# Three edits to a two-block transformer kernel on one core: wide FFN matmuls, 64-row scores, differential attention filled in pieces

## Chip, core and metric

One NeuronCore of a Trainium2 chip runs the whole program in one launch. The metric is the device time of that launch in microseconds (us); lower is better. The kernel is written in Python with a tile framework, which orders the instructions of each engine when it builds the program. The engines are TensorE (PE, its weight loads PEld), VectorE (DVE), ScalarE (ACT), GpSimd (POOL) and SyncE (SP, which issues the DMAs). Each takes its instructions strictly in the order in which they stand, except that PE may load weights ahead.

## The reference, cut to what matters

`x` is 256 tokens of width 1024, `ctx` another 256. The first block mixes by convolution and retention, then has a feed forward (2816 wide) and a gated side input. The second block has two layers over `x` and `ctx`. The parts that the change touches:

```python
f = (silu(h @ w_ffn_gate) * (h @ w_ffn_up)) @ w_ffn_down        # block 1; layer 2 of block 2 has the same form, x alone
# layer 1 of block 2: differential attention, 8 heads, each of two 64-wide halves m
s = einsum('bqhmd,bkhmd->bhmqk', q_blk, k) * 64 ** -0.5
p = softmax(s);  p = p[:, :, 0] - lam * p[:, :, 1];  o = p @ v   # x attends to ctx and x, ctx to ctx
y = (rmsnorm(o) * subln * 0.8) @ wo                              # norm per head
# layer 2 of block 2: neighbourhood attention, 16 heads of 64, x alone as queries
s = concat([q @ k_band * 64 ** -0.5 + bias, q @ k_ctx * 64 ** -0.5]);  o = softmax(s) @ v
```

All is float32.

## The kernel before

**Number format.** A float32 matrix is held as two parts, `hi` (rounded to the format float32r that PE multiplies in one pass) and `lo` (the rest). A product is three float32r matmuls per 128-row slice k of the contraction: weight hi by x hi, weight hi by x lo, weight lo by x hi (`mm3`, lines 156 to 163; `mm3_tok`, lines 165 to 172, has the tokens as the stationary side). Each of the three loads its own 128x128 weights. Weights come from memory as float32; `weights` (line 121) loads a tile `raw` of 128x1024, ACT casts it to `hi` (line 129) and DVE subtracts to get `lo` (line 130). Four `raw` and five `hi` and `lo` buffers let this run ahead of PE.

**Feed forwards.** The one of block 1 (22 steps j, lines 563 to 588) and the one of layer 2 (lines 1107 to 1118) have 256 tokens. Per j, gate and up are each 8 slices k of `mm3` with 256 (or, in layer 2, 258) columns; the result is scaled on DVE out of PSUM (line 574, line 1113), ACT takes silu, DVE multiplies, and `split` (line 146) makes the two parts. In layer 2 two extra columns carry the shift of the norm, and the scale of the norm is multiplied in afterwards. `down` (line 590) then takes 22 slices k per output block n, eight blocks. The feed forward of layer 1 (lines 965 to 985) has x and ctx side by side, 512 columns, and is not touched. Into these stages the framework also moves `ada_dve` (line 243): 320 multiplies of 128x512 on DVE that make the modulation vectors and are needed only later.

**Differential attention** (lines 725 to 866). For each c of 4, q, k and v of two heads are projected from `xl` (x) while the parts of `ctx` were done earlier for c below 3 (`early_qk`, `early_v`, line 637). `rope` (line 728) is four DVE operations of 256 columns. Then come 8 units (`da_unit`, line 744), 32 in all: one head, one half of 128 queries, over 512 keys (x queries) or 256 keys (ctx queries). A unit is two score matmuls `s` of 64 contraction rows, one for each half m, on plain float32 (line 757); per m a maximum on DVE (761), its scaling by -1/8 (762) and the exponential on ACT (764); the combination on DVE (767 to 770); transposes on PE (773); a copy by ACT (775); the products with v (780); the norm of the head (783 to 787, with one `pow` on POOL); and a transpose `on` that is put off by one unit (`flush`, 742). The two score banks of PSUM (`pss`) are the only two. The output projection by the first six heads, for x (`wo_first(0)`, line 901), stands after all units.

**Neighbourhood attention** (lines 983 to 1077). A score `s` of a head and 128 queries is two matmuls: one of 128 rows, in which the other head's 64 rows hold the low part of q (line 989), and one of 64 rows for the low part of k (line 990). To make these packed tiles q and k are copied in halves of 64 partitions (lines 1039 to 1041 and 1069 to 1070).

**Order.** The framework chooses the order on each engine by a model of its own, within data dependencies and the hints `tc.issue_after(x)` (not before x).

Of the kernel before, what the change touches and what calls it, by code (L numbers as in the profile page):

```python
# [35 lines left out]
EARLYN = 9  # L36
# [25 lines left out]
def body(ctx, tc, a):  # L62
# [91 lines left out]
    last_mm = [None]  # L154

    def mm3(out, w, xs, first=True, last=True):
# [408 lines left out]
    rc_ = stc.rstd()  # L565
    ada = AdaPE(ADA_PE)
    fs = []
    for j in range(KF):
        w = w_blocks(a["ffn1"][j])
        ps = bank(pmm, "mm")  # L570
        for i in range(2):
            mm3(ps[:, i * T:(i + 1) * T], w[i], xs)
        gu = tmp2()
        op = dve.tensor_tensor(
            gu.rearrange("p (j t) -> p j t", j=2), ps.rearrange("p (j t) -> p j t", j=2),
            rx[:, :T].unsqueeze(1).to_broadcast([P, 2, T]), op=ALU.mult)
        if j == 1:
            in_ffn = last_load[0], op.ins
        sg = tmp1()
        act.activation(sg, gu[:, :T], AF.Silu)  # L580
        dve.tensor_tensor(sg, sg, gu[:, T:], op=ALU.mult)
        s = slot("x" if ring(j) == "pt" else ring(j), F32R)
        split(sg, s[:, :T], s[:, T:])
        fs.append((s[:, :T], s[:, T:]))
# [5 lines left out]
    def down(name, fs, epilogue):  # L590
        for n in range(KD):
            ps = bank(pmm, "mm")
            for hf in range(2):
                w = per_k(weights(a[name][2 * n + hf], (6 * P, 5 * P)), (6, 5), P)
                mm3(ps[:, :T], w, fs[hf * KH:(hf + 1) * KH], first=hf == 0, last=hf == 1)
            epilogue(n, ps)
# [25 lines left out]
    def ep(n, ps):  # L622
# [9 lines left out]
        st.add(ps[:, :T])  # L632
# [3 lines left out]
        act.activation(s[:, (n % 2) * T:(n % 2 + 1) * T], ps[:, :T], AF.Copy, scale=col(V_FFNPOST, n))  # L636
# [3 lines left out]
    early = [], [], []  # L640

    def early_qk(c, grp):
        w = w_blocks(a["wqkv0"][grp * 4 + c])
        ps = bank(pss, "s")
        for j in range(2):
            o = ps[:, j * T:(j + 1) * T]
            mm3(o, w[j], xc)
            if c < 2:
                s = slot("q")
                act.copy(s[:, T:], o)  # L650
                early[c].append(s)
        if c == 2:
            s = slot("o")
            act.copy(s, ps)
            early[c].append(s)

    def early_v(c):
# [4 lines left out]
        s = slot("q" if c < 2 else "o")  # L662
        act.copy(s, ps)
        early[c].append(s)

    steps = [lambda c=c, i=i: early_v(c) if i == 2 else early_qk(c, i) for c in range(3) for i in range(3)][:EARLYN]

# [49 lines left out]
    epsc = const.tile([P, 1], F32, name="epsc")  # L717
    dve.memset(epsc, EPS)
# [4 lines left out]
    dve.tensor_scalar(out=sub8, in0=col(V_SUBLN), scalar1=1.0 - LAM_INIT, scalar2=None, op0=ALU.mult)  # L723
# [21 lines left out]
    def da_unit(q, k, v, hh, ctx_q, qt, po_all, at):  # L745
# [7 lines left out]
        p, ps = [], []  # L753
# [505 lines left out]
```

## Time and profile before

| what | value |
|---|---|
| three runs | 1449.93, 1446.19, 1448.93 us; median 1448.93 |
| the profiled execution: time | 1450.36 us |
| its span, first to last instruction | 1448.1 us |
| PE, weight loads, DVE, ACT, POOL busy | 97%, 87%, 74%, 48%, 2% |
[...]
| chain that ended last | PE 80%, issue 13%, DMA 2%, DVE 2%, ACT 1% |
| DMA | 163 GB/s mean, its engines about half busy |

How to read it: matmuls are pipelined and the profile models their ends, so a matmul row of 0.28 us overlaps its successors, and PE reads as busy as soon as matmuls follow each other closely. What a matmul costs PE is seen in the start of the next one. The stages lie, from the span's start, about so: block 1 up to its feed forward 0 to 162, feed forward 162 to 350, the rest of block 1 and the early projections to 442, differential attention to 643, layer 1's output and feed forward to 1060, neighbourhood attention to 1240, its output and feed forward to the end.

### The profile page before, as it was taken

Reading aid. Unit: us, or ns where it says so; the run is one execution under the profiler, and the core shown is the slowest. Engines: PE = TensorE matmul, PEld = TensorE weight load, DVE = VectorE, ACT = ScalarE, POOL = GpSimd, SP = SyncE. Lnnn points to the kernel's source line nnn. Section 1 sums busy time; section 2 is a strip of 40 time slices with the busy share of each in tenths; the row PEclk is TensorE's granted clock in tenths of the full one; section 3 lists DMA queues with packets and bytes.
Section 4 is the critical chain, followed back from the end, with each engine's and each line's share of the span. In section 5 each row is a group of like instructions: output and inputs, shape, how many; then the busy total and the mean of one; then the engine's idle time right before and its main releaser. Section 6 shows DMA issues by size and latency. Waiting matters only on the chain.

```text
span 1448.1 us, 25617 instructions
## 1 busy us (share of the span) xinstructions
PE 1410.9 (97%) x9811; PEld 1262.8 (87%) x9811; DVE 1075.4 (74%) x2333; ACT 700.5 (48%) x1323; POOL 34.1 (2%) x52
## 2 busy tenths in 40 slices
PE   7998999999999999999999999999999999999997
PEld 6898899999998887589888888889988778899997
DVE  7975889985778785778699999965775576676653
ACT  5655544454554545754432222323565555654442
POOL 0000000000000010110000000000000000000000
PEclk9999899999999999999999999999999999999998
DMA  8457498677554331034466676634632233355562
GB/s 289 128 168 255 169 318 275 218 215 221 167 175 146 131 96 32 7 103 160 132 215 198 210 239 218 210 123 129 203 99 87 74 88 119 132 182 182 153 180 91
DMA packets 76874, 236.66 MB, mean 163 GB/s; under 512 B 8656, under 2 KB 13008, under 8 KB 76624
## 3 DMA queue, kind: packets, MB, share of 16 engines
q1 hardware_dynamic: 76752, 235.03, 50.6%
q8 instruction: 77, 1.26, 0.3%
q14 instruction: 45, 0.37, 0.1%
HBM read 233.95 MB, written 1.05 MB: 162 GB/s over the span
## 4 chain that ended last, share of the span: by engine, by line
PE 80%; issue 13%; DMA 2%; DVE 2%; ACT 1%; SPq 0%; POOL 0%; DVEq 0%; POOLq 0%; ACTq 0%
PE mm L161 19%; PE mm L162 19%; PE mm L163 19%; PE s L757 3%; PE mm L172 2%; PE mm L171 2%; PE mm L170 2%; PE t L780 2%; PE o L1022 1%; DMA raw<-w_in 1%; PE s L162 1%; PE s L161 1%; PE s L163 1%; PE t L1012 1%; PE s L990 1%
## 5 line engine op out<-in xcount | busy, mean ns | idle before, releaser
L129 ACT CAST hi<-raw 128x1024 fp32r<-128x1024 f32 (+2 forms) x376 | 358.8, 956 | 547.8 <-PE mm L162 345.7
L130 DVE TENSOR_TENSOR lo<-raw,hi 128x1024 fp32r<-128x1024 f32 (+2 forms) x376 | 415.5, 1106 | 158.1 <-ACT hi L129 154.6
L161 PE MATMUL mm<-x,hi 128*128 128x256 f32 (+2 forms) x1568 | 486.3, 314 | 13.0 <-ACT x L151 7.9
L162 PE MATMUL mm<-x,hi 128*128 128x256 f32 (+2 forms) x1568 | 487.4, 312 | 1.3 <-DVE x L612 1.0
L163 PE MATMUL mm<-x,lo 128*128 128x256 f32 (+2 forms) x1568 | 487.5, 312 | 0.8 <-DVE lo L130 0.8
L161 PEld LDWEIGHTS mm<-x,hi 128*128 128x128 f32 x1568 | 299.9, 193 | 39.7 <-issue 11.4
L163 PEld LDWEIGHTS mm<-x,lo 128*128 128x128 f32 x1568 | 301.9, 193 | 23.5 <-issue 8.6
L162 PEld LDWEIGHTS mm<-x,hi 128*128 128x128 f32 x1568 | 301.9, 193 | 22.2 <-issue 6.1
L256 DVE SCALAR_TENSOR_TENSOR junk<-adaw,sb 128x512 f32<-128x512 f32 x320 | 220.2, 688 | 12.9 <-DMA adaw<-ada 8.5
L161 PE MATMUL mm<-o,hi 128*128 128x256 f32 (+1 forms) x356 | 105.3, 300 | 0.7 <-ACT o L147 0.5
L162 PE MATMUL mm<-o,hi 128*128 128x256 f32 (+1 forms) x356 | 105.6, 298 | 0.0
L163 PE MATMUL mm<-o,lo 128*128 128x256 f32 (+1 forms) x356 | 105.3, 297 | 0.0
L163 PE MATMUL s<-x,lo 128*128 128x258 f32 (+1 forms) x288 | 81.9, 284 | 0.0
L161 PE MATMUL s<-x,hi 128*128 128x258 f32 (+1 forms) x288 | 81.8, 284 | 0.0
L162 PE MATMUL s<-x,hi 128*128 128x258 f32 (+1 forms) x288 | 81.8, 284 | 0.0
L162 PE MATMUL mm<-q,hi 128*128 128x256 f32 (+1 forms) x265 | 81.0, 306 | 0.0
L163 PE MATMUL mm<-q,lo 128*128 128x256 f32 (+1 forms) x265 | 80.9, 305 | 0.0
L161 PE MATMUL mm<-q,hi 128*128 128x256 f32 (+1 forms) x265 | 80.9, 305 | 0.0
L161 PEld LDWEIGHTS mm<-o,hi 128*128 128x128 f32 x356 | 67.4, 191 | 5.4 <-issue 1.7
L162 PEld LDWEIGHTS mm<-o,hi 128*128 128x128 f32 x356 | 68.0, 191 | 2.6 <-issue 0.5
L163 PEld LDWEIGHTS mm<-o,lo 128*128 128x128 f32 x356 | 68.0, 191 | 1.9 <-issue 0.2
L172 PE MATMUL mm<-hi,x 128*128 128x256 f32 x240 | 69.1, 288 | 0.0
(250 smaller groups left out, 2153.9 us busy)
## 6 DMA issues: line engine op xcount, KB each, us to landing
raw<-gu SPq DMA_DIRECT2D x88, 512.0 KB, 3.9
adaw<-ada SPq DMA_DIRECT2D x80, 512.0 KB, 4.5
raw<-wqkv SPq DMA_DIRECT2D x66, 512.0 KB, 4.3
raw<-ffn SPq DMA_DIRECT2D x44, 512.0 KB, 5.6
raw<-down SPq DMA_DIRECT2D x37, 384.0 KB, 3.2
raw<-down SPq DMA_DIRECT2D x37, 320.0 KB, 3.0
raw<-w_in SPq DMA_DIRECT2D x22, 512.0 KB, 5.3
o<-ada SPq DMA_DIRECT2D x32, 256.0 KB, 5.9
```

The source lines that it names most:

```text
L129: last_conv[:] = [act.copy(hi[:, :n], raw[:, :n]).ins, dve.tensor_tensor(lo[:, :n], raw[:, :n], f32(hi[:, :n]), op=ALU.subtract).ins]
L130: dve.tensor_tensor(lo[:, :n], raw[:, :n], f32(hi[:, :n]), op=ALU.subtract).ins]
L161: pe.matmul(out, wh, xh, start=first and k == 0, stop=False)
L162: pe.matmul(out, wh, xl, start=False, stop=False)
L163: last_mm[0] = pe.matmul(out, wl, xh, start=False, stop=last and k == n - 1).ins
L170: pe.matmul(out, xh[:, ts_], wh, start=k == 0, stop=False)
L171: pe.matmul(out, xh[:, ts_], wl, start=False, stop=False)
L172: pe.matmul(out, xl[:, ts_], wh, start=False, stop=k == n - 1)
L256: dve.scalar_tensor_tensor(out=junk, in0=raw[:, gs_], scalar=1.0, in1=sb[:, v, gs_], op0=ALU.mult, op1=ALU.mult, accum_out=acc[:, n, v, g: ...
L757: pe.matmul(o, q[ms, qs], k[ms, k0:k0 + n], start=True, stop=True)
L780: mm = pe.matmul(po[:, :P], pT[:, j * P:(j + 1) * P], vv, start=j == 0, stop=j == nk - 1)
L990: pe.matmul(ps, q[rows, qs], k[2][rows], start=False, stop=True)
```

## The change

Three edits. In the two 256-token feed forwards, after the first few steps j, x is normalized (and modulated) beforehand and its two parts stand side by side in one 512-column tile, so weight hi takes both in one matmul of 512 columns and weight lo takes the hi part in one of 256; the two halves of the PSUM bank are added when it is read (`halves`, a `tensor_reduce` over the halves). The first steps (4 in block 1, 3 in layer 2) keep the old form while DVE and ACT make the normalized x. `down` does the same for 7 of 8 output blocks. Second, the scores of both attentions become three float32r matmuls of 64 rows for each m or head, in pairs for the two row halves; q and k are split into hi and lo in one piece, and 1/8 goes into q. Third, the projections of differential attention are cut into pieces (`qk_piece`, `v_piece`, `early_piece` for the ctx part of c = 3, `wo_piece`) and each is put behind the scores of a given unit. Beside these, the negation of the maximum goes into the reduction, and part of the head norm's arithmetic goes to POOL.

```diff
-EARLYN = 9
+WO_AT = {1: (0,), 2: (1, 2), 3: (3,), 4: (4,), 5: (5,), 6: (6,), 7: (7,)}
+WIDE1, XN1 = 4, 3
+WIDE2 = 3
+    def both_free(mm):
+        if last_exp[0] is not None:
+            tc.add_manual_dep(mm.ins, last_exp[0].name, ...)
+    def mm3_wide(out, w, xs, first=True, last=True):
+        n = len(xs)
+        for k in range(n):
+            (wh, wl), x = w[k], xs[k]
+            end = last and k == n - 1
+            if end:
+                pe.matmul(out[:, :T], wl, x[:, :T], start=False, stop=False)
+            last_mm[0] = pe.matmul(out, wh, x, start=first and k == 0, stop=end).ins
+            if not end:
+                last_mm[0] = pe.matmul(out[:, :T], wl, x[:, :T], start=False, stop=False).ins
+    def halves(ps):
+        t = tmp1()
+        dve.tensor_reduce(out=t, in_=ps.rearrange("p (j t) -> p t j", j=2), axis=AX.X, op=ALU.add)
+        return t
...
+        else:
+            pg, pu = bank(pmm, "mm"), bank(pss, "s")
+            mm3_wide(pg, w[0], xn)
+            mm3_wide(pu, w[1], xn)
+            g, u = halves(pg), halves(pu)
...
+        for k in range(j * XN1, min(KD, (j + 1) * XN1)):
+            t = tmp1()
+            dve.tensor_tensor(t, h[k], rx[:, :T], op=ALU.mult)
+            x = slot("x", F32R)
+            split_scaled(t, col(V_FFNPRE, k), x[:, :T], x[:, T:])
+            xn.append(x)
...
+                if n == KD - 1:
+                    mm3(ps[:, :T], w, [(s[:, :T], s[:, T:]) for s in xs], first=hf == 0, last=hf == 1)
+                else:
+                    mm3_wide(ps, w, xs, first=hf == 0, last=hf == 1)
+            epilogue(n, ps[:, :T] if n == KD - 1 else halves(ps))
...
-            pe.matmul(o, q[ms, qs], k[ms, k0:k0 + n], start=True, stop=True)
+        for i, (a_, b_) in enumerate(((qh, kh), (qh, kl), (ql, kh))):
+            for m in range(2):
+                ms = slice(64 * m, 64 * m + 64)
+                mm = pe.matmul(ps[m], a_[ms, qs], b_[ms, k0:k0 + n], start=i == 0, stop=i == 2)
+                if i + m == 0:
+                    both_free(mm)
...
-            dve.tensor_reduce(out=sc[:, m:m + 1], in_=o, axis=AX.X, op=ALU.max)
-            dve.tensor_scalar(out=sc[:, 2 + m:3 + m], in0=sc[:, m:m + 1], scalar1=-0.125, scalar2=None, op0=ALU.mult)
+            dve.tensor_reduce(out=sc[:, 2 + m:3 + m], in_=o, axis=AX.X, op=ALU.max, negate=True)
...
+        pool.tensor_tensor(sc[:, 6:7], sc[:, 4:5], sc[:, 4:5], op=ALU.mult)
-        dve.scalar_tensor_tensor(out=sc[:, 6:7], in0=sc[:, 4:5], scalar=sc[:, 4:5], in1=epsc, op0=ALU.mult, op1=ALU.mult)
-        dve.scalar_tensor_tensor(out=sc[:, 10:11], in0=sc[:, 9:10], scalar=1.0 / 128, in1=sc[:, 6:7], op0=ALU.mult, op1=ALU.add)
+        pool.tensor_scalar(out=sc[:, 10:11], in0=sc[:, 6:7], scalar1=128 * EPS, scalar2=sc[:, 9:10], op0=ALU.mult, op1=ALU.add)
...
+    def qk_piece(c, grp, j):
+        def run(ins):
+            part_ = weights(a["wqkv0"][grp * 4 + c][:, j * 1024:(j + 1) * 1024], (1024,))
+            ps = bank(pmm, "mm")
+            with behind(ins):
+                mm3(ps[:, :T], per_k(part_, [KD], P), xl)
+            ring_ = "q" if (c, j) == (3, 1) else "o"
+            raw, hi, lo = tmp2(), slot(ring_, F32R), slot(ring_, F32R)
+            act.copy(raw[:, T:], early[c][grp][:, j * T:(j + 1) * T])
+            rope(raw, ps[:, :T])
+            if grp == 0:
+                split_scaled(raw, 0.125, hi, lo)
+            else:
+                split(raw, hi, lo)
+            QK[c][grp][j] = (hi, lo)
+        return run
...
+    for c in range(3):
+        fill = {0: [qk_piece(c, 0, 1)], 1: [qk_piece(c, 1, 1)], 4: [qk_piece(c + 1, 0, 0)], 5: [qk_piece(c + 1, 1, 0)]}
+        if c == 0:
+            fill.update({2: [early_piece(0, 0)], 3: [early_piece(0, 1)], 6: [v_piece(1, 0)], 7: [v_piece(1, 1)]})
...
+        da_heads(c, fill)
...
+    da_heads(3, {u: [wo_piece(0, n) for n in ns] for u, ns in WO_AT.items()})
...
-        pe.matmul(ps, q[:, qs], k[jj], start=True, stop=False)
-        pe.matmul(ps, q[rows, qs], k[2][rows], start=False, stop=True)
+        for n, (a_, b_) in enumerate(((qh, kh), (qh, kl), (ql, kh))):
+            for jj in range(2):
+                rows = slice(64 * jj, 64 * jj + 64)
+                mm = pe.matmul(ps[jj], a_[rows, qs], b_[rows], start=n == 0, stop=n == 2)
+                if n + jj == 0:
+                    both_free(mm)
```

What the change does to the order, at three places. First PE, in the last heads of differential attention before the change (`s` scores of one m, `t<-tab,e` transposes, `t<-o,pt` products with v, `o<-tab,on` the late transposes):

```order
L757 MATMUL s<-q 128x256
L757 MATMUL s<-q 128x512
L773 MATMUL t<-tab,e 128x128 x2
L757 MATMUL s<-q 128x512
L780 MATMUL t<-o,pt 128x128 x2
L742 MATMUL o<-tab,on 128x128
L773 MATMUL t<-tab,e 128x128 x2
L757 MATMUL s<-q 128x512
L780 MATMUL t<-o,pt 128x128 x2
L757 MATMUL s<-q 128x512
```

Here the scores of the two halves m stand apart, with nothing of the projections between. After the change PE stands so in the middle of the same attention (L796 is the score line, L199 and L170 to L172 are projection pieces):

```order
L197 MATMUL mm<-hi,x 128x256
L198 MATMUL mm<-lo,x 128x256
L199 MATMUL mm<-hi,x 128x256
L796 MATMUL s<-o 128x512 x6
L170 MATMUL mm<-x,hi 128x256
L171 MATMUL mm<-x,hi 128x256
L172 MATMUL mm<-x,lo 128x256
```

The six score matmuls of a unit stand together in all 32 units. Between two units' scores stand 18 to 48 matmuls of projections, most often 24; in one place 15 and in one, where c = 3 begins, none. Second DVE, in the feed forward of block 1, before the change (L574 scales gate and up together, L256 is `ada_dve`):

```order
L574 TENSOR_TENSOR t_2996<-mm,rstd 128x512
L256 SCALAR_TENSOR_TENSOR junk,adacc<-adaw,sb 128x512
L130 TENSOR_TENSOR lo<-raw,hi 128x1024
L581 TENSOR_TENSOR t_2998<-t_2998,t_2996 128x256
L256 SCALAR_TENSOR_TENSOR junk,adacc<-adaw,sb 128x512
L130 TENSOR_TENSOR lo<-raw,hi 128x1024
L148 TENSOR_TENSOR o<-t_2998,o 128x256
L256 SCALAR_TENSOR_TENSOR junk,adacc<-adaw,sb 128x512
```

and after it (L189 is `halves`, L132 the weights' `lo`, L283 `ada_dve`):

```order
L616 TENSOR_TENSOR t_2528<-t_2528,t_2565 128x256
L189 TENSOR_REDUCE t_2631<-mm 128x256
L283 SCALAR_TENSOR_TENSOR junk,adacc<-adaw,sb 128x512
L132 TENSOR_TENSOR lo<-raw,hi 128x1024
L189 TENSOR_REDUCE t_2633<-s 128x256
L132 TENSOR_TENSOR lo<-raw,hi 128x1024
L150 TENSOR_TENSOR q<-t_2528,q 128x256
```

Two reductions take the place of one multiply per step, and fewer `ada_dve` stand between: 41 against 64 from the first product of this feed forward to its last. Third DVE in differential attention after the change (L803 is the maximum, L769 to L772 `rope`, L154 the split of q):

```order
L803 TENSOR_REDUCE sc<-s 128x1 x2
L772 TENSOR_TENSOR t_6367<-rp 128x256
L809 RECIPROCAL sc<-sc 128x1
L769 STREAM_SHUFFLE rp<-mm 128x256
L770 TENSOR_TENSOR rp<-mm,tab 128x256
L810 SCALAR_TENSOR_TENSOR sc<-sc,nlam 128x1
L771 TENSOR_TENSOR rp<-rp,tab 128x256
L803 TENSOR_REDUCE sc<-s 128x1 x2
L811 SCALAR_TENSOR_TENSOR e<-e,sc 128x512
L154 SCALAR_TENSOR_TENSOR o<-t_6367,o 128x512
```

In 22 of the 32 units the two maxima stand together, in the others one or two operations apart. From one unit's to the next stand 4 to 15 operations, most often six to eight, three of them the unit's own (L809 to L811).

## Rows read from the trace of the kernel before

**Rows 1.** The page: engines' busy time, and the chain that ended last.

```profile
PE 1410.9 (97%) x9811; PEld 1262.8 (87%) x9811; DVE 1075.4 (74%) x2333; ACT 700.5 (48%) x1323; POOL 34.1 (2%) x52
PE 80%; issue 13%; DMA 2%; DVE 2%; ACT 1%; SPq 0%; POOL 0%; DVEq 0%; POOLq 0%; ACTq 0%
```

**Rows 2.** Windows: us; PE, PEld, DVE, ACT, POOL busy (instructions); clock; DMA share, GB/s.

```profile
162.00:288.00 126.00, 126.00 (x1030) 117.40 (x1030) 115.38 (x242) 58.86 (x88) 1.54 (x1) 1.00 0.82 277
442.00:643.00 201.00, 197.24 (x1282) 155.25 (x1281) 151.12 (x454) 116.28 (x314) 18.01 (x31) 1.00 0.28 85
575.00:625.00 50.00, 46.85 (x261) 31.11 (x261) 36.80 (x115) 34.66 (x104) 5.94 (x11) 1.00 0.18 54
850.00:875.00 25.00, 25.00 (x112) 20.72 (x111) 23.36 (x57) 6.89 (x8) 0.00 (x0) 1.00 0.73 234
1300.00:1325.00 25.00, 25.00 (x210) 25.00 (x209) 17.70 (x27) 12.16 (x18) 0.00 (x0) 1.00 0.56 181
```

**Rows 3.** Timeline of PE, single scores: start us, duration us, what.

```profile
502.37 0.28 PE L162 MATMUL mm<-x,hi 128*128 128x256 f32 x1
502.58 0.70 PE L757 MATMUL s<-q 64*128 64x256 f32 x2
503.21 0.39 PE L163 MATMUL mm<-x,lo 128*128 128x256 f32 x1
...
511.95 0.28 PE L161 MATMUL mm<-x,hi 128*128 128x256 f32 x1
512.16 1.12 PE L757 MATMUL s<-q 64*128 64x512 f32 x2
513.21 0.71 PE L780 MATMUL t<-q,pt 128*128 128x128 f32 x4
```

**Rows 4.** Timeline of PE, two scores that stand together.

```profile
580.92 0.70 PE L757 MATMUL s<-q 64*128 64x256 f32 x4
581.55 0.66 PE L773 MATMUL t<-tab,e 128*128 128x128 f32 x4
```

**Rows 5.** Timeline of PE, neighbourhood attention: 128 rows, then 64, then 128 again.

```profile
1088.87 0.39 PE L989 MATMUL s<-q 128*128 128x512 f32 x1
1089.19 0.50 PE L990 MATMUL s<-q 64*128 64x512 f32 x1
1089.62 0.39 PE L162 MATMUL mm<-x,hi 128*128 128x256 f32 x1
```

**Rows 6.** Groups by line and form, DVE: xcount, busy us, mean ns, idle before.

```profile
L574 DVE TENSOR_TENSOR t<-mm,rstd 128x512 f32<-128x512 f32 x22 | 15.1, 687 | 1.4 <-PE mm L163 1.4
L761 DVE TENSOR_REDUCE sc<-s 128x1 f32<-128x512 f32 x32 | 22.1, 689 | 9.1 <-PE s L757 8.2 <-POOL sc L785 0.8
L130 DVE TENSOR_TENSOR lo<-raw,hi 128x1024 fp32r<-128x1024 f32 x242 | 295.6, 1223 | 94.2 <-ACT hi L129 91.5 <-PE o L285 0.7
L581 DVE TENSOR_TENSOR t<-t,t 128x256 f32<-128x256 f32 x22 | 9.2, 420 | 0.0
L762 DVE TENSOR_SCALAR sc<-sc 128x1 f32<-128x1 f32 x64 | 9.4, 148 | 0.3
```

**Rows 7.** Timeline of DVE: how closely its operations follow each other.

```profile
509.59 1.22 DVE L130 TENSOR_TENSOR lo<-raw,hi 128x1024 fp32r<-128x1024 f32 x1
510.73 0.16 DVE L767 RECIPROCAL sc<-sc 128x1 f32<-128x1 f32 x1
...
510.86 0.69 DVE L761 TENSOR_REDUCE sc<-s 128x1 f32<-128x512 f32 x1
511.46 0.68 DVE L256 SCALAR_TENSOR_TENSOR junk<-adaw,sb 128x512 f32<-128x512 f32 x1
```

**Rows 8.** Timeline, all engines: from a score to the next that needs its bank.

```profile
585.83 0.43 DVE L761 TENSOR_REDUCE sc<-s 128x1 f32<-128x256 f32 x1 [0.83 <-PE s L757]
586.54 0.47 ACT L764 ACTIVATE e<-s,sc 128x256 f32<-128x256 f32 x1 [0.51 <-DVE sc L762]
587.16 1.12 PE L757 MATMUL s<-q 64*128 64x512 f32 x2 [0.56 <-ACT e L764]
```

More of the change, by code (lines that the diff above doesn't have):

```diff
@@ L789, in da_unit, with behind @@
         late.append((po_all[:, at:at + P], on))
-    os_, raws = [], []
-    def da_heads(c, q, k, v):
+        return last_s
+    QK = [[[None] * 2 for _ in range(2)] for _ in range(4)]
+    V = [[] for _ in range(4)]
+    def behind(ins):
+        return tc.issue_after(ins) if ins is not None else nullcontext()
+    def qk_piece(c, grp, j):
+        def run(ins):
+            part_ = weights(a["wqkv0"][grp * 4 + c][:, j * 1024:(j + 1) * 1024], (1024,))
+            ps = bank(pmm, "mm")
+            with behind(ins):
[10 more added lines that the diff above has]
+        return run
@@ new lines, in body, with v_piece, run, early_piece @@
+    open_v = [None]
+    def v_piece(c, jj):
+        def run(ins):
+            if jj == 0:
+                open_v[0] = bank(pmm, "mm"), w_wide(a["wqkv0"][8 + c])
+            ps, w = open_v[0]
+            with behind(ins):
+                mm3_tok(ps[:, jj * T:(jj + 1) * T], w, xl, CS[jj])
+            if jj == 1:
+                s = slot("q")
+                act.copy(s, ps)
+                V[c] += [s, early[c][2]]
+        return run
+    open_e = [None]
+    def early_piece(i, j):
+        def run(ins):
+            if j == 0:
+                src = a["wqkv0"][i * 4 + 3]
+                open_e[0] = bank(pmm, "mm"), w_wide(src) if i == 2 else w_blocks(src)
+            ps, w = open_e[0]
+            o = ps[:, j * T:(j + 1) * T]
+            with behind(ins):
+                if i == 2:
+                    mm3_tok(o, w, xc, CS[j])
+                else:
+                    mm3(o, w[j], xc)
+            if j == 1:
+                s = slot("q")
+                act.copy(s, ps)
+                early[3].append(s)
+        return run
@@ L794, in da_heads, with split_raws, fill_in @@
+    os_, raws = [], []
+    def split_raws():
+        for raw in raws:
+            hi, lo = slot("x", F32R), slot("x", F32R)
+            split(raw, hi, lo)
+            os_.append((hi, lo))
+        raws.clear()
+    def da_heads(c, fill):
+        def fill_in(u, ins):
+            for f in fill.get(u, ()):
+                f(ins)
         if c == 3:
-            parts = [(slot("o", F32R), slot("o", F32R)) for _ in range(2)]
+            parts = [(slot("x", F32R), slot("x", F32R)) for _ in range(2)]
+            u = 0
@@ L898, in down_half, with wo_piece, run @@
                 between()
+    open_w = [None]
+    def wo_piece(v, n):
+        def run(ins):
+            if n % 2 == 0:
+                open_w[0] = weights(a["wo0a"][n // 2], (768, 768)), bank(pmm, "mm")
+            ws, ps = open_w[0]
+            o = ps[:, (n % 2) * T:(n % 2 + 1) * T]
+            with behind(ins):
+                mm3(o, per_k([ws[n % 2]], (6,), P), part(os_[:6], v))
+            resid(0, 2, n, o, v)
+        return run
     def wo_first(v):
         for n in range(KD):
[L902 to L909 removed]
+            wo_piece(v, n)(None)
+    da_heads(3, {u: [wo_piece(0, n) for n in ns] for u, ns in WO_AT.items()})
     sts = (Stat(T), Stat(T))
@@ L1064, in body @@
                 mm3(ps, wk[j], xs)
[L1066 to L1070 removed]
+            s = slot("q", F32R), slot("q", F32R)
+            split(ps, *s)
             k.append(s)
```

248 lines of the change are left out of this document (108 added, 140 removed).

## Prediction

> **What bounds the kernel now.** I read the page first: PE is busy for 97% of the span, the chain that ended last is PE for 80% of it, and DVE, the next, is at 74% [rows 1]. That only names the engine; what a matmul costs it is seen from stretches. Where PE does nothing but 256-column matmuls it starts 210 of them in 25 us, 0.119 us each; with 512 columns it starts 112, 0.223 each [rows 2]. Each start has its own weight load beside it, so two 256-column matmuls cost 0.238 us where one of 512 costs 0.223: a matmul costs its columns and about 0.015 more. [...] The kernel is then nearly a sum of matmul starts, with three kinds of exception: waits at the norms, which the change does not touch; 64-row matmuls, which cost more than their columns; and a part of differential attention, from 575 to 625 us, where PE has nothing to do for 3 us of 50 and starts 261 matmuls where a dense stretch starts 420 [rows 2].
>
> **The change part by part.**
>
> *Wide matmuls.* Per slice k, three 256-column matmuls (3 x 0.119 = 0.357) become one of 512 and one of 256 (0.223 + 0.119 = 0.342): 0.015 us saved [rows 2]. The columns streamed are the same, 768; only one weight load goes. There are 18 x 16 = 288 slices in the first feed forward, 19 x 16 = 304 in the second and 7 x 22 = 154 in each `down`: 900 in all, 13.5 us. Lower end 0, should the 256-column matmul after a wide one pay for the load that the wide one hid; upper end 13.5 again, since no row shows a cheaper 256.
>
> What this adds is on DVE: 88 `halves` of 512 inputs. The trace has no reduction that reads two halves of a bank in turn. The nearest rows are the contiguous reduction of 512 at 0.689 us and the 512-wide multiply at 0.687 [rows 6]; I take 0.69, with the 1.22 us of a 1024-element operation as the far end, should each pair of elements cost two steps. Operations follow each other 0.08 us closer than they last (0.60 for 0.69, 1.14 for 1.22) [rows 7]. Per new step in the first feed forward DVE then has two `halves`, two weights, a multiply and a split of 256 (0.34 each, for 0.42 [rows 6]): 1.20 + 2.28 + 0.68 = 4.16 us. Over the stage: 18 x 4.16, four old steps at 3.56 (one multiply of 512 for two `halves`), 41 `ada_dve` at 0.61 (the order has moved 23 behind the stage) and 16 operations of 256 for the normalized x, together 120 us. PE's 126 us of [rows 2] hold 1030 matmuls, 21 steps of 48 and one for the modulation, 6.0 us each; 22 of them less 18 x 16 x 0.015 are 128. Before, DVE was busy for 115 of those 126 us, and PE did not wait. So I cost it at nothing, hidden under the matmuls; the margin is 8 us, and if it is gone, PE pays what DVE is over. The normalized x is made three blocks per step under the old steps. The last output block of `down` keeps the old form, so the end of the stage is not longer.
>
> [...]
>
> *Scores of differential attention.* One plain float32 score of 512 keys moves the next matmul from 511.95 + 0.12 to 513.21, so it costs 1.14 us; one of 256 costs 503.21 - 502.37 - 0.12 = 0.72 [rows 3]. There are 32 of each: 59.5 us. Six times two stand together and overlap: in one such place both are done in 0.63 us, what one alone takes [rows 4], so about 0.65 x 6 = 4 us come off: 55.5. After the change a unit goes into 64-row work once. Going in and out costs 0.32 - 0.22 = 0.10 before and 0.43 - 0.22 = 0.21 after, by the 64-row score of neighbourhood attention [rows 5]; I take 0.30 for both. Between lie three pairs; the two row halves overlap as in [rows 4], so 3 x 0.223 for 512 keys and 3 x 0.119 for 256. That is 0.97 and 0.66 a unit, 16 of each, 26 us: **30 us saved**. If pairs do not overlap: 16 x (0.30 + 6 x 0.223) + 16 x (0.30 + 6 x 0.119) = 42.5, 13 saved. The order shows all six together in each unit, so the first holds if the hardware does for float32r what it did for float32.
>
> *Scores of neighbourhood attention.* Before, 32 x (0.32 + 0.43) = 24 us [rows 5]. After, 16 visits of 0.97, and in four places the order puts transposes inside a visit, which costs 0.5 more each: 17.5. **6.5 us saved**; without overlap 4 lost. The half-partition copies that go were on ACT and DVE beside PE's work: nothing on the path.
>
> *Filling.* The same columns are projected as before; c = 3 has its weights loaded, cast and subtracted a second time for ctx (six tiles, 7 us of DVE, 3 MB), in a stage whose DMA is at 28% [rows 2]. On DVE the 64 scalings of maxima go, 0.148 each [rows 6], and 64 other operations on single columns, which I count alike: 19 us. 16 splits of 512 at 0.69 and six weights at 1.22 come: 18. So DVE keeps its 151 us of the stage [rows 2], in 201 - 30 = 171: 88%, close to full but below the 23.4 of 25 that it holds in layer 1's feed forward while PE does not wait there [rows 2]. What filling can give back is PE's idle time in 575 to 625, about 3 us [rows 2], and waits of a quarter microsecond that the modelled ends of matmuls hide; I allow 7 us in all. What it can take: the next unit's scores now need both banks at once, and behind them on PE wait the projections. I set the two against each other, 0, with -7 and +16 (half a microsecond a unit) as ends. POOL gets two more small operations a unit; only the late transpose, a unit later, waits for them.
>
> *Sum.* 13.5 + 30 + 6.5 = 50. The profiled execution took 1450.4 us (2.3 above its span, 1.4 above the median of the three runs): **1400 us**, and 1399 against the median.
>
> **The rivals.**
>
> *The bank turnaround becomes the bound (slower than before).* From a score's maximum to the next score that may use its bank, 1.33 us passed with 256 keys and an idle DVE [rows 8]. With 512 keys and two maxima: 0.69 + 0.60, an exponential of some 0.7 (0.47 for 256 [rows 8]) and half a microsecond for its sum and for handing over make 2.5 us. Fill between two units is 24 x 0.119 and some ten transposes and products at 0.11: 3.9 us, so 1.4 us are spare. DVE takes its work in order: if weights (1.22), a split (0.69), `rope` (four of about 0.42) stand ahead of the maxima, 3.6 us, PE waits 2.2 us a unit, 70 us in all, and the time is 1470. It decides from 1.6 us a unit on (50/32). For it: DVE at 88%, and in units with a q or k piece, the 512-key ones, its work exceeds PE's. Against it: the units between have little DVE work, the pieces are needed only three or four units later, and the order puts the maxima early. At a third of the price, 0.7 us a unit, 1422.
>
> *Pairs don't overlap.* 13.5 + 13 - 4 = 22.5 saved: 1428. Against it stands [rows 4], where both banks and both row halves ran at once.
>
> *`halves` costs double.* DVE in the first feed forward is then 120 + 36 x 0.54 = 139 us against PE's 128, 11 to 13 us lost there; in the second 5.2 per step against 5.5, nothing or little: 1413. [...]
>
> *The wide form saves nothing.* If the load is not what the 0.015 us is made of, or the next load shows behind the shorter matmul, 1414.
>
> **How the numbers follow.** Forecast, all three terms within a few us (1388 to 1410): 0.62. `halves` double (0.09) or the wide form for nothing (0.06), 1411 to 1418: 0.15. Turnaround at part price (1412 to 1440): 0.09. No overlap: 0.05. Turnaround at about 50 us, which eats the whole gain: 0.03. Turnaround beyond that, slower: 0.05. Faster still: 0.01. A measurement of this kernel can tell 0.3%, 4.3 us. So faster 0.92, same 0.03, slower 0.05. The range goes from 1386, where filling also ends the waits of the stage and a little more, to 1428, which takes in `halves`, no overlap and the part price.
>
> **What would show it.** In the feed forwards, starts alternating 0.22 and 0.12 us apart, some 143 to 147 matmuls in 25 us, `halves` near 0.69 us and DVE below 95%. In differential attention, the six score matmuls in pairs that start together, about 1.0 us from the first to the next other matmul with 512 keys, and the stage near 171 us. Wrong would be: pairs one behind the other; idle time of PE before scores that ends with the exponential on ACT, in most units; `halves` at 1.2 us; a 256-column matmul after a wide one that takes over 0.12 us.

## The result and the profile after

| | before | after |
|---|---|---|
| median | 1448.40 us (4 runs) | 1426.89 us (4 runs, 1426.06 to 1429.95) |
| the profiled execution: time, span | 1450.36, 1448.1 us | 1429.95, 1428.2 us |
| mean granted TensorE clock | 0.991 | 0.980 |

The ratio is 0.9856, 95% interval 0.9836 to 0.9877: 21.5 us faster, where some 49 were forecast. The page of the kernel after, busy time and the chain that ended last, against [rows 1]:

```profile
PE 1377.8 (96%) x9007; PEld 1217.4 (85%) x9007; DVE 1097.1 (77%) x2238; ACT 701.2 (49%) x1330; POOL 63.8 (4%) x116
PE 78%; issue 14%; DVE 3%; ACT 2%; DMA 2%; POOL 1%; SPq 0%; DVEq 0%; POOLq 0%; ACTq 0%
```

804 matmul records are gone (a plain float32 matmul, as the scores were before, has two: x2 in [rows 3]), and yet PE's share of the chain fell while those of DVE, ACT and POOL rose: PE now waits for them. Windows of the kernel after, with the columns of [rows 2]:

```profile
250.00:275.00 25.00, 25.00 (x144) 21.74 (x143) 24.16 (x48) 12.26 (x18) 0.00 (x0) 1.00 0.66 220
325.00:350.00 25.00, 20.77 (x104) 17.74 (x103) 23.41 (x55) 13.19 (x25) 0.00 (x0) 0.86 0.66 207
375.00:400.00 25.00, 22.18 (x174) 21.91 (x173) 18.18 (x35) 12.62 (x22) 0.69 (x1) 0.93 0.34 105
425.00:450.00 25.00, 22.13 (x167) 21.73 (x167) 18.27 (x34) 14.00 (x24) 0.70 (x1) 0.89 0.52 170
450.00:475.00 25.00, 21.15 (x146) 19.19 (x144) 15.60 (x32) 11.68 (x21) 0.39 (x2) 0.83 0.32 103
1300.00:1325.00 25.00, 25.00 (x144) 21.75 (x143) 20.33 (x28) 12.39 (x19) 0.00 (x0) 1.00 0.56 187
```

The first and last are wide feed forwards: full clock, PE without a gap. The four between lie in the first down projection and around the norms behind it. There PE idles 3 to 4 us of 25, and the granted clock, 1.00 in all four before the change, is 0.83 to 0.93. In the first of the four it is 0.50 from 340.21 to 345.46 us; 0.86 over 25 us is some 7 us at that level.

The table cuts the profiled execution of each kernel at the same marks: the start of the `pow` on POOL in a norm, and the end of the last `silu` of the first feed forward (us). The last five kernels are experiments, told below.

| stage | before | after | wide_only | no_wide | gate_old | cover | best |
|---|---|---|---|---|---|---|---|
| start, to the norm of feed forward 1 | 159.2 | 160.5 | 157.7 | 158.8 | 155.1 | 156.6 | 156.1 |
| gate and up of feed forward 1 | 132.5 | 130.3 | 130.2 | 132.4 | 132.2 | 130.2 | 132.1 |
| its down, early projections, differential attention, to layer 1's norm | 390.8 | 383.8 | 396.0 | 376.6 | 376.8 | 375.6 | 362.4 |
| layer 1's feed forward | 339.9 | 339.7 | 340.1 | 339.9 | 339.7 | 340.0 | 339.8 |
| neighbourhood attention, to its norm | 233.7 | 224.1 | 233.7 | 224.1 | 224.0 | 224.0 | 224.0 |
| feed forward of layer 2, to the end | 192.0 | 189.8 | 189.7 | 191.6 | 189.8 | 189.4 | 187.6 |

Each column is one execution; that of the change was the slowest of its four, that of `best` the fastest. The first stage, which no edit touches, differs by up to 5 us from column to column. Layer 1's feed forward, which no edit touches either, agrees within 0.4 here, but with the kernels that are not shown it goes from 338.8 to 341.0, so a difference of one or two us in a single stage says little. Of the 32 us forecast for the third stage only 7 came.

### The profile page after: what moved, and what is told of

Read it like the earlier page. It is cut to its first block, busy times and chain, and to the rows that moved or that the text cites. A ratio compares the mean times of both kernels' runs of the same rounds, so it can differ in the third digit from the quotient of the medians.

```text
span 1428.2 us, 23983 instructions
## 1 busy us (share of the span) xinstructions
PE 1377.8 (96%) x9007; PEld 1217.4 (85%) x9007; DVE 1097.1 (77%) x2238; ACT 701.2 (49%) x1330; POOL 63.8 (4%) x116
## 4 chain that ended last, share of the span: by engine, by line
PE 78%; issue 14%; DVE 3%; ACT 2%; DMA 2%; POOL 1%; SPq 0%; DVEq 0%; POOLq 0%; ACTq 0%
PE mm L170 16%; PE mm L171 15%; PE mm L172 15%; PE mm L182 5%; PE s L182 2%; PE mm L184 2%; PE mm L197 2%; PE mm L198 2%; PE mm L199 2%; PE s L796 1%; PE o L1134 1%; PE t L821 1%; PE s L171 1%; PE s L172 1%; PE s L170 1%
## 5 line engine op out<-in xcount | busy, mean ns | idle before, releaser
L132 DVE TENSOR_TENSOR lo<-raw,hi 128x1024 fp32r<-128x1024 f32 (+2 forms) x382 | 421.9, 1106 | 154.7 <-ACT hi L131 152.5
L170 PE MATMUL mm<-x,hi 128*128 128x256 f32 (+2 forms) x1120 | 361.3, 328 | 14.8 <-ACT x L153 8.0
L171 PE MATMUL mm<-x,hi 128*128 128x256 f32 (+2 forms) x1120 | 362.4, 325 | 1.3 <-DVE x L658 1.3
L172 PE MATMUL mm<-x,lo 128*128 128x256 f32 (+2 forms) x1120 | 361.9, 325 | 0.8 <-DVE lo L132 0.8
L170 PEld LDWEIGHTS mm<-x,hi 128*128 128x128 f32 x1120 | 216.4, 196 | 39.1 <-issue 9.8
L172 PEld LDWEIGHTS mm<-x,lo 128*128 128x128 f32 x1120 | 218.5, 195 | 18.4 <-issue 3.4
L171 PEld LDWEIGHTS mm<-x,hi 128*128 128x128 f32 x1120 | 218.4, 195 | 17.4 <-issue 1.7
L283 DVE SCALAR_TENSOR_TENSOR junk<-adaw,sb 128x512 f32<-128x512 f32 x320 | 219.7, 687 | 11.0 <-DMA adaw<-ada 6.5
L182 PE MATMUL mm<-x,hi 128*128 128x512 f32 x200 | 73.0, 399 | 0.0
L170 PE MATMUL mm<-o,hi 128*128 128x256 f32 (+1 forms) x228 | 68.9, 311 | 2.4 <-ACT o L149 2.1
L197 PE MATMUL mm<-hi,x 128*128 128x256 f32 x240 | 70.3, 293 | 0.0
L172 PE MATMUL mm<-o,lo 128*128 128x256 f32 (+1 forms) x228 | 69.5, 307 | 0.0
L171 PE MATMUL mm<-o,hi 128*128 128x256 f32 (+1 forms) x228 | 69.4, 306 | 0.0
L199 PE MATMUL mm<-hi,x 128*128 128x256 f32 x240 | 69.3, 289 | 0.0
L198 PE MATMUL mm<-lo,x 128*128 128x256 f32 x240 | 69.0, 288 | 0.0
L182 PE MATMUL s<-x,hi 128*128 128x512 f32 x144 | 52.6, 397 | 0.0
L170 PEld LDWEIGHTS mm<-o,hi 128*128 128x128 f32 x228 | 43.3, 194 | 5.9 <-ACT o L149 2.8
```

The lines of the kernel that those rows point to most:

```text
L132: dve.tensor_tensor(lo[:, :n], raw[:, :n], f32(hi[:, :n]), op=ALU.subtract).ins]
L182: last_mm[0] = pe.matmul(out, wh, x, start=first and k == 0, stop=end).ins
L197: pe.matmul(out, xh[:, ts_], wh, start=k == 0, stop=False)
L198: pe.matmul(out, xh[:, ts_], wl, start=False, stop=False)
L199: pe.matmul(out, xl[:, ts_], wh, start=False, stop=k == n - 1)
L283: dve.scalar_tensor_tensor(out=junk, in0=raw[:, gs_], scalar=1.0, in1=sb[:, v, gs_], op0=ALU.mult, op1=ALU.mult, accum_out=acc[:, n, v, g: ...
```

## Experiments

### Which part gave the gain: one part alone, one part undone

`wide_only` is the kernel before with `mm3_wide`, `halves` and what calls them; `no_wide` is the kernel after with those lines put back. `plain_scores` has the old scores of differential attention in the order of the change:

```diff
-        for i, (a_, b_) in enumerate(((qh, kh), (qh, kl), (ql, kh))):
-            for m in range(2):
...
+        for m in range(2):
+            mm = pe.matmul(ps[m], q[ms, qs], k[ms, k0:k0 + n], start=True, stop=True)
```

> The kernel before with the wide feed forwards alone (gate and up after the first steps, seven blocks of both down projections). Theory: the wide slices save 0.010 us each, 9 us over 900, but the first down projection now waits for DVE, which reads its banks behind the norm of ctx and the modulation products, and PE then runs at half clock for a while, 7 us back: 1443 to 1450 us, no more than 5 below before, with a PE wait of several us before a wide matmul between 320 and 350 us. Rival (wide is worth its forecast, the loss of the whole lies in the filling): 1435 us, no such wait.

Measured: 1448.40 us, ratio 1.0001 (0.9992 to 1.001). The theory holds: no gain at all. The wait stands at 332.7 us, 4.4 us long (counted, as in what follows, from start to start less the usual distance; the profile, which models where matmuls end, prints 4.23), and the third stage is 5.2 us longer than before, about what the two feed forwards gained (2.3 each).

> The change with all wide matmuls undone: scores, filling and the rest alone. Theory: within 5 us of the whole change, 1422 to 1432 us. Rival (the wide form gives its 13.5 us and the rest fell short): about 1440 us.

Measured: 1423.26 us, ratio 0.9826 (0.981 to 0.9843), 3.6 us below the change. Two of the three edits carry the whole gain, and the first takes some back.

> The change with the scores of differential attention back as one plain float32 matmul per half m, the two standing together behind one wait (no split of q and k, 1/8 in the exponential again). Theory: most of the gain of the scores comes from the two halves standing together; a pair of plain ones costs what one costs, 1.14 us for 512 keys and 0.65 for 256, against 0.92 and 0.62 for three pairs: 4 us more than the change, 1429 to 1433 us, DVE having less to do. Rival (the three float32r passes are what saves): 20 us or more above the change, from 1447 us on.

Measured: 1436.92 us, ratio 0.9926 (0.9899 to 0.9952): 10 above the change, between the two. Visit by visit the theory holds: a pair of plain scores costs PE 1.15 us with 512 keys and 0.72 with 256, where three pairs cost 0.99 and 0.64, 3.8 us over 32 units. Where the other 6 us lie was not separated. There is a wait of 3.0 us at 594.5, and half of the sixteen 256-key visits take 0.8 to 1.4 us from the first score to the next other matmul, where an undisturbed one takes 0.63; which of the added operations makes them wait was not tried. By the rows of undisturbed visits, that two halves which stand together cost what one costs brings the 55.5 us of visits before down to 16 x (1.15 + 0.72) = 30 by itself, most of what the term claimed.

### The wait in the first down projection

PE of the kernel after, where the seventh output block follows the sixth:

```profile
335.58 0.39 PE L182 MATMUL mm<-o,hi 128*128 128x512 f32 x1
340.21 0.77 PE L182 MATMUL mm<-q,hi 128*128 128x512 f32 x1 [4.23 <-DVE t L189]
340.77 0.41 PE L184 MATMUL mm<-q,lo 128*128 128x256 f32 x1
340.98 0.63 PE L182 MATMUL mm<-q,hi 128*128 128x512 f32 x1
```

and DVE up to then (L268 makes the modulation, L654 and L658 are the norm of ctx, L189 is `halves`):

```profile
330.19 0.18 DVE L268 SCALAR_TENSOR_TENSOR mod<-mod,vec 128x16 f32<-128x16 f32 x1
330.40 1.27 DVE L654 SCALAR_TENSOR_TENSOR t<-hc,mod,rstd 128x256 f32<-128x256 f32 x3
...
338.98 0.48 DVE L654 SCALAR_TENSOR_TENSOR t<-hc,mod,rstd 128x256 f32<-128x256 f32 x1
339.38 0.68 DVE L189 TENSOR_REDUCE t<-mm 128x256 f32<-128x512 f32 x1
339.98 0.87 DVE L658 SCALAR_TENSOR_TENSOR x<-t,mod,x 128x256 fp32r<-128x256 f32 x2
```

Before the change the modulation was ready 40 us earlier (L241):

```profile
289.76 0.18 DVE L241 SCALAR_TENSOR_TENSOR mod<-mod,vec 128x16 f32<-128x16 f32 x1
```

The norm of ctx (emitted behind block 2, `XCAT`) cannot begin until the modulation is made, now at 330.2, and the framework put three `halves` of finished blocks behind it on DVE. All three banks were full until 339.4. After the wait the matmuls ran at half clock (0.50 granted): the next twenty took 5.9 us instead of 3.5. Four kernels ask what is at fault. `down1_old` returns this projection to `mm3`, so that ACT reads its banks; `gate_old` returns gate and up instead (`WIDE1, XN1 = KF, 0`); `xcat5` moves the norm (`XCAT = 5`); `warm` adds 36 matmuls that nobody reads ahead of the waiting block:

```diff
+                if name == "down1" and (n, hf) == (6, 0):
+                    pd = bank(pst, "t")
+                    with tc.issue_after(last_mm[0]):
+                        for _ in range(36):
+                            pe.matmul(pd[:, :T], xs[0][:, :P], xs[0][:, :T], start=True, stop=True)
```

> The change with the first down projection alone back in the old form, so ACT and not DVE reads its banks. Theory: the wait of 4.4 us before a matmul of this projection and the half clock behind it go, 1.7 us of wide matmuls are given back: about 1421 us, 4 to 8 below the change. Rival (DVE's queue is only late elsewhere then: the norm behind it waits instead): 1426 to 1430 us.

Measured: 1428.98 us, ratio 0.9868 (0.9851 to 0.9885). The theory falls, and the rival is nearer: the wait is there still, now 6.6 us, and ends with ACT. PE and ACT of this run (L657 is the norm of ctx, L682 reads the banks):

```profile
333.27 0.58 PE L170 MATMUL mm<-q,hi 128*128 128x256 f32 x1 [6.46 <-ACT x L682]
```
```profile
331.17 0.91 ACT L657 ACTIVATE x<-t,mod 128x256 fp32r<-128x256 f32 x2 [0.68 <-DVE t L654]
332.35 0.51 ACT L657 ACTIVATE x<-t,mod 128x256 fp32r<-128x256 f32 x1 [0.28 <-DVE t L654]
332.77 1.18 ACT L682 ACTIVATE x<-mm,vec 128x256 f32<-128x256 f32 x3
```

On ACT, too, the readers of three banks stand behind the norm of ctx. So it does not matter who reads; what matters is how late that norm is.

> The change with gate and up of the first feed forward alone in the old form; its down projection stays wide, so DVE reads its banks. Theory (the backlog comes from the 36 halves and the 41 instead of 64 modulation products beside gate and up, whoever reads the banks of down): no wait over 1 us in the down projection, 7 us less, 2.3 us of wide matmuls given back: 1421 to 1424 us. Rival (it is the halves in down that wait behind the norm of ctx): the wait stays, 1429 us.

Measured: 1420.06 us, ratio 0.9803 (0.9789 to 0.9818), one below the theory's figure, though `halves` still reads these banks. With gate and up in the old form 64 modulation products stand beside them again, not 41, the modulation is made at 285.3 us instead of 330.2, and nothing waits:

```profile
325.00:350.00 25.00, 25.00 (x170) 22.98 (x169) 23.30 (x49) 14.30 (x21) 0.00 (x0) 1.00 0.77 254
```

> The change with the norm of ctx (16 operations on DVE, 8 on ACT) and the modulation products ahead of it put behind block 5 of the first down projection instead of block 2. Theory (the readers of the banks stand behind this norm, which waits for a late modulation): the wait of 4.4 us and the half clock behind it, 2.6 us, shrink to under 2 together: 1420 to 1423 us. Rival (DVE's backlog moves on): the early projections or the first norm wait instead, 1425 to 1430 us.

Measured: 1420.66 us, ratio 0.9807 (0.9792 to 0.9822): the wait is gone, 6.2 us gained. But the waits around the first norm grew from 3.1 to 5.3 us, so part of the rival is right as well: a late DVE is late at the next place that asks for it.

> The change with 36 matmuls of 256 columns into a bank that nobody reads, put on TensorE ahead of the seventh block of the first down projection, where the change waits 4.4 us for DVE. Theory: they take 4.3 us of the wait, the granted clock stays at 1.00 in 325 to 350 us, and the twenty matmuls behind the wait, which took 0.30 us each, take 0.18: 2.5 us less, 1424.5 us. Rival (the half clock has another cause, such as the load of DVE or of memory): the twenty matmuls stay at 0.30 us, 1427 us.

Measured: 1421.69 us, ratio 0.9818 (0.9803 to 0.9832). The window and the rows behind the added matmuls (L641; the view begins at the fourth of them):

```profile
325.00:350.00 25.00, 25.00 (x173) 23.11 (x173) 24.30 (x52) 15.28 (x27) 0.00 (x0) 1.00 0.66 213
```
```profile
330.83 4.11 PE L641 MATMUL t<-q 128*128 128x256 f32 x33
334.87 0.47 PE L182 MATMUL mm<-q,hi 128*128 128x512 f32 x1
335.18 0.28 PE L184 MATMUL mm<-q,lo 128*128 128x256 f32 x1
335.30 0.40 PE L182 MATMUL mm<-q,hi 128*128 128x512 f32 x1
```

The clock stays at 1.00, and the twenty matmuls take 3.5 us instead of 5.9. DVE and memory are as busy as in the change (24.30 us of 25 against 23.41, and a DMA share of 0.66 in both), so PE's own idleness is what lowered the clock there; the 2.4 us are shown by the rows. The total fell by 5.2; the rest lies farther on, where the framework ordered the pieces ahead of the first score differently (PE's wait there is 2.4 us in this kernel, 3.6 in the change), and was not separated.

### The norms and the first score

Three norms lie between the down projection and differential attention. PE of the kernel after: the first of them and the third (L249 is the broadcast behind a norm's sums), and the first score:

```profile
377.82 0.71 PE L249 MATMUL t<-tab,rv 128*128 128x128 f32 x4 [1.16 <-POOL rv L214]
380.19 1.01 PE L170 MATMUL mm<-o,hi 128*128 128x256 f32 x3 [1.66 <-ACT o L149]
...
441.42 0.60 PE L249 MATMUL t<-tab,rv 128*128 128x128 f32 x4
443.61 0.50 PE L170 MATMUL mm<-x,hi 128*128 128x256 f32 x2 [1.58 <-ACT x L657]
444.07 0.28 PE L198 MATMUL mm<-lo,x 128*128 128x256 f32 x1
445.64 0.58 PE L171 MATMUL mm<-x,hi 128*128 128x256 f32 x1 [1.29 <-DVE x L658]
446.02 0.41 PE L172 MATMUL mm<-x,lo 128*128 128x256 f32 x1
...
459.21 0.28 PE L199 MATMUL mm<-hi,x 128*128 128x256 f32 x1
463.05 0.79 PE L796 MATMUL s<-o 64*128 64x512 f32 x2 [3.56 <-ACT o L149]
```

Before the change PE had early projections of ctx to do in these places: around the first norm the order was 48 of their matmuls, the sums, 24, the broadcast, 72; now all 144 stand ahead of the sums and nothing behind. The edit that made `early_qk` copy a bank once, instead of half by half, is what moved them: with two copies, as in `cover` below, where no hint acts on these three pieces, the order is 48, sums, 48, broadcast, 48. What took the cover from the third norm was not tried by itself. At the first score the split of q and k stands on DVE between weights of later pieces (L132), which the old order did not ask for at this point (L154 and L150 are the splits):

```profile
460.20 1.21 DVE L132 TENSOR_TENSOR lo<-raw,hi 128x1024 fp32r<-128x1024 f32 x1
461.33 0.68 DVE L154 SCALAR_TENSOR_TENSOR o<-t,o 128x512 fp32r<-128x512 f32 x1
...
462.27 1.22 DVE L132 TENSOR_TENSOR lo<-raw,hi 128x1024 fp32r<-128x1024 f32 x1
463.40 0.68 DVE L150 TENSOR_TENSOR o<-t,o 128x512 fp32r<-128x512 f32 x1
```

`cover` only changes that order (`last_stat` and `bc2` are the last sum and the second norm's broadcast, `held()` the hint `issue_after`):

```diff
-        s = slot("q")
-        act.copy(s, ps)
+            if j == 0:
+                s = slot("q")
+            act.copy(s[:, j * T:(j + 1) * T], ps[:, j * T:(j + 1) * T])
...
-    early_some(EARLY[1] if EARLY[1] is not None else EARLY[0], 99)
+    early_some(3, 5)
+    hold[0] = bc2
+    early_some(5, 7)
+    hold[0] = last_stat[0]
+    early_some(7, 8)
...
+    hold[0] = last_mm[0]
+    for f in (v_piece(0, 0), v_piece(0, 1)):
+        f(hold[0])
+    early_some(8, 99)
```

> The change with the order of the early projections of ctx held: in each piece the halves are copied out one by one again (so that two pieces of 48 matmuls stand around the first norm instead of none), pieces 6 and 7 stand behind the second norm's broadcast, piece 8 behind the third norm's sums, piece 9 behind the first q and k pieces. Nothing else is changed, no work added. Theory (the scores' gain was lost where the norms and the first score lost their cover): the PE waits of 1.3, 1.8, 1.7, 1.5 and 3.6 us from 376 to 463 us go and with them most of the stretches at half clock, 12 us or more: 1412 to 1417 us; the wait of 4.4 us near 335 us stays. Rival (the loss is in DVE's load of the filled units): the waits turn up in later units, 1424 us or more.

Measured: 1417.59 us, ratio 0.9785 (0.9769 to 0.9801): 9.3 us off the change with no work changed; the theory's 12 us or more did not come, and the time is just above its range. The waits at the first norm and the first score are gone (450 to 475 below), but the hints made new ones, 1.9 and 3.4 us ahead of the third norm's sums:

```profile
400.00:425.00 25.00, 21.14 (x175) 20.73 (x174) 17.65 (x34) 14.51 (x27) 0.70 (x1) 1.00 0.51 172
425.00:450.00 25.00, 22.65 (x160) 22.28 (x161) 15.89 (x36) 10.43 (x19) 0.70 (x1) 0.86 0.29 89
450.00:475.00 25.00, 25.00 (x198) 22.84 (x198) 20.38 (x41) 17.59 (x39) 3.49 (x6) 1.00 0.50 165
```

> The change without any wide matmul and with the order of the early projections held as in the run named cover. Theory: the waits at the norms and the first score are the scores' and filling's own, so the 9.3 us between the change and cover come off here too, 1414 to 1416 us; and wide matmuls are worth what separates this from cover and from cover_xcat5: nothing or a loss of some 3 us with the late norm of ctx, nothing without it. Rival (the wide form makes DVE late at the norms): only 3 to 5 us come off, 1418 to 1420 us.

Measured: 1418.66 us, ratio 0.9801 (0.9784 to 0.9818), 4.6 below `no_wide`: the rival's figure. By the third stage, which leaves the scatter of the start out, the gains are closer: 8.2 us from the change to `cover`, and 6.5 from `no_wide` to this kernel (376.6 to 370.1). The waits at the norms are the same in the change and in `no_wide` (that before the first score is 1.1 us shorter there), so most of the gain is the order's own; whether the wide form adds to these waits is not settled by so small a difference. `cover` is 1 us below this kernel, which is within the scatter, and `cover_xcat5` 3 us, so wide matmuls are worth little here; the norm of ctx was not moved without them.

> Both edits of the two runs named cover and xcat5. Theory: the gains add, 1405 to 1411 us, near the forecast. Rival (both are one backlog): no more than 3 us under the better of the two.

Measured: 1415.64 us, ratio 0.9772 (0.9758 to 0.9787): only 2 below `cover`, the rival's case. The wait in the down projection is gone, the two ahead of the third norm's sums stay, and a new one of 1.5 us stands behind the first norm: DVE's backlog has moved on.

### The filling itself

`free_fill` drops the hint that puts each piece behind its unit's scores (`behind` returns no hint). The work is the same.

> The change without the hint that holds each projection piece behind the scores of its unit: same work, but TensorE now finds 0 to 13 projection matmuls between two units' scores in 13 places (most of them in the second half of the attention) and 25 to 65 in the others. Theory (the bank turnaround of the prediction's first rival is real, 2.5 us with 512 keys, and the filling of 24 matmuls hides it): each of the thin places costs PE 1 to 2 us, 13 to 20 us in all with what the clock takes: 1438 to 1448 us, with waits before scores that end with the exponential or the maximum. Rival (the turnaround is hidden by transposes and products in any order): 1424 to 1431 us.

Measured: 1441.71 us, ratio 0.9963 (0.9949 to 0.9977): 14.8 us slower than the change, the theory's figure, but not by its mechanism: the place of the price was another. The worst window, and the largest waits of PE in 560 to 660 us (engine, line, what it waited for, us in total, times, longest):

```profile
575.00:600.00 25.00, 19.55 (x78) 13.97 (x75) 17.90 (x51) 11.86 (x39) 5.22 (x14) 0.52 0.11 37
```
```profile
PE t L821 <- ACT pt L816: 5.6, 6, 1.4
PE o L780 <- ACT on L828: 1.9, 2, 1.4
PE t L814 <- DVE e L811: 1.9, 2, 1.1
PE s L796 <- ACT e L805: 1.2, 4, 0.5
```

Where no projections stand between two units, PE waits for the unit's own chain (exponentials, combination, transposes, copy), hardly for the score bank (1.2 us in all), and the granted clock falls to half, 0.52, for a whole window.

### A version that beats both

`best` puts together what the runs had shown: gate and up of feed forward 1 old, the held order, the wide form of feed forward 2 from step 5, and one early projection more:

```diff
-WIDE1, XN1 = 4, 3
-WIDE2 = 3
+WIDE1, XN1 = KF, 0
+WIDE2 = 5
...
+    steps.insert(8, lambda: early_qk(3, 0))
...
-    early_some(5, 7)
+    early_some(5, 8)
...
-            fill.update({2: [early_piece(0, 0)], 3: [early_piece(0, 1)], ...
+            fill.update({2: [early_piece(1, 0)], 3: [early_piece(1, 1)], ...
```

> The change with gate and up of the first feed forward in the old form, the wide form of the second feed forward from step 5 on instead of 3, the held order of the early projections, and a tenth early projection (q of ctx for c = 3, so that the others of c = 3 move up one place in the filling). Theory: cover's 1417.6 less 6.8 for the wait in the first down projection, less 2 for the waits of the second feed forward for its normalized x, less 3 to 5 for the norms' remaining waits: 1402 to 1408 us. Rival (each wait that goes turns up at the next norm): 1411 us or more.

Measured: 1405.72 us (1403.76 to 1406.70), ratio 0.9711 (0.9695 to 0.9727): 41.8 us below before and 21 below the change. Its page, and the two windows that were worst in the change:

```profile
PE 1368.2 (98%) x9327; PEld 1225.0 (87%) x9327; DVE 1080.6 (77%) x2204; ACT 700.5 (50%) x1329; POOL 66.3 (5%) x116
```
```profile
325.00:350.00 25.00, 25.00 (x167) 22.83 (x167) 23.10 (x47) 13.61 (x19) 0.00 (x0) 1.00 0.77 254
450.00:475.00 25.00, 25.00 (x202) 22.76 (x202) 21.73 (x49) 17.10 (x46) 6.24 (x12) 1.00 0.38 126
```

PE is back at 98% and the mean clock at 0.991. The waits of feed forward 2 for its normalized x (0.4, 0.8 and 1.0 us between 1243 and 1253 in the change) are gone too, and so are those ahead of the third norm's sums that `cover` had made: PE idles 4.9 us between 400 and 425 in `cover_no_wide`, and not at all here. It is the tenth early projection that took these away, and not the earlier modulation, since `cover_no_wide` makes the modulation as early (at 287.2 us, here at 286.2).

## Why the prediction was right and wrong

*Scores: right, to the tenth.* PE of the kernel after, one unit of either length in differential attention and one of neighbourhood attention:

```profile
485.39 0.96 PE L796 MATMUL s<-o 64*128 64x512 f32 x6
486.28 0.39 PE L170 MATMUL mm<-x,hi 128*128 128x256 f32 x1
...
500.13 0.62 PE L796 MATMUL s<-o 64*128 64x256 f32 x6
500.68 0.39 PE L197 MATMUL mm<-hi,x 128*128 128x256 f32 x1
...
1145.92 0.96 PE L1094 MATMUL s<-q 64*128 64x512 f32 x6
1146.81 0.39 PE L170 MATMUL mm<-x,hi 128*128 128x256 f32 x1
```

Six matmuls in 0.89 us of starts, 0.99 and 0.64 with going in and out: 0.97 and 0.66 were forecast. Undisturbed, 32 visits cost 26 us, as the prediction said, and the pairs overlap as in [rows 4]. One reading was off: of the six pairs before, only one of 256 keys (the row shown) and the one of 512 overlapped in full; the other four, of 256 keys, took 1.06 to 1.08 us, not 0.63, so the visits before cost about 1 us more than the 55.5. In neighbourhood attention visits fell from 25.0 to 17.4 us (24 and 17.5 forecast); the stage gained 9.6, of which 2 stay unexplained.

*Wide matmuls: right in kind, too large.* A slice fell from 0.360 to 0.351 us, start to start, not by 0.015: the 512-column matmul starts 0.235 before its 256-column one, not 0.223 as among its like [rows 2], and the 256 takes 0.117. That is 8.1 us over 900 slices, 5.4 less than the term.

*`halves`: right.* Groups of DVE in the kernel after, `halves` and the contiguous maximum of as many elements:

```profile
L189 DVE TENSOR_REDUCE t<-mm 128x256 f32<-128x512 f32 x51 | 34.9, 686 | 6.8 <-PE mm L182 5.3
L803 DVE TENSOR_REDUCE sc<-s 128x1 f32<-128x512 f32 x32 | 20.9, 683 | 4.2 <-PE s L796 3.8 <-POOL sc L826 0.5
```

Reading two halves of a bank in turn costs 0.686 us against 0.683, and the rival in which it doubles is dead.

*The step that failed* is the one on what the wide form adds on DVE: "So I cost it at nothing, hidden under the matmuls; the margin is 8 us". The sum of 120 us for that stage was good: DVE was busy for 120.4 of its 130.3 us, and PE had no wait in it. But it came out only because 23 modulation products moved behind the stage, and those were not followed to where they went. The modulation was made at 330.2 us, before the change at 289.8; the norm of ctx came about as much later, and three bank readers stand behind it on each engine that could read. Price: 4.4 us of wait and 2.4 of half clock, 7.0 by `gate_old` in the third stage. That one step cost nearly what the wide form brought, and `wide_only` is level with before.

*A second step failed in the same way, and cost more.* The prediction set waits at the norms aside as something "which the change does not touch", and set filling's give and take to 0. It looked at the order in the stages that the diff edits, not at the early projections, whose copy the diff also changes. Their cover for the norms went, and the split and more weights stand between the first q and k and the first score. `cover` got 8.2 us of the third stage back, which is shown. The tenth piece of `best` got about 6 more: its third stage is 362.4 us, where `cover` with the 7.0 of `gate_old` would have 368.6, and where `cover_no_wide` with the 1.4 that wide matmuls save in the down projection would have the same; no kernel adds that piece alone. The shortfall is 30 us between the two profiled spans (28 between the medians). In the prediction's terms it is then 5.4 (slices), 7 (down projection), 14 (norms and first score, 8 of them by `cover` alone) and 2 (waits for the normalized x), less 3 that neighbourhood attention gave more; 1.3 lie in the first stage, which is scatter, and some 3 remain open. They may lie in the filled units, whose give and take was set to 0: behind the first, six of the 32 visits took 0.1 to 1.3 us longer than undisturbed ones, 4.6 us together.

*The rivals.* The bank turnaround came in three of the 32 units only: PE waited 0.70, 0.84 and 0.58 us for an exponential at 480.6, 575.6 and 601.1. `free_fill` shows that the filling has 15 us at stake, on the unit's chain rather than on the bank. The time came out near the third of the turnaround's price, 1422, and just inside the stated range, but by another mechanism: that is luck. What would show the forecast wrong was listed as waits before scores in most units; it should have listed a clock below 1.00 in stretches where it had been 1.00.

## What to carry to other kernels

Where a change makes an off-path engine fuller in one stage, follow the work that the scheduler pushes out of that stage to the place where it lands, and ask who stands behind it in order on each engine. A small edit of a copy can move the work that covers a latency somewhere else; compare the order around every norm, not only in the edited stages. Here two scores on the two row halves of the array that stood together undisturbed cost what one costs (0.63 us with 256 keys, [rows 3] and [rows 4]): by the rows of undisturbed visits, bringing them together was worth most of this change's gain on the scores.

## What the runs showed of the hardware

Waits were dearer than their length. In the change, behind a wait of 4.4 us and behind two of 1.6 and 1.3 us that stand close together, matmuls ran at a granted clock of 0.50 for 5 to 6 us (340.21 to 345.46 and 445.64 to 451.40; the one of 256 columns at 446.02 lasts 0.41 us, the one at 444.07, between the two waits, 0.28); with matmuls that nobody reads in the wait, the clock stayed at 1.00 (`warm`, 325 to 350 us). What a wait of that length costs was not the same in every run: `plain_scores` also has 4.2 us of PE idle in 325 to 350 us, and there the granted clock of that window is 0.93, where it is 0.86 in the change. The prediction left the clock out of its sum; it was 1.00 in the stretches it read [rows 2], but of each new wait it should have asked what that would do to the clock.
